# A chunked scan in 64-wide tiles: the level products of the triangular inverse kept inside one layout

## The chip, the core and the metric

The kernel runs on one core of a Trainium2 chip as one program. The metric is the device time of that program in microseconds, the median of the runs; before the change it is 4052.07 us (three runs, 4046.66 to 4060.16).

## The reference, cut to what matters

The program is two stacked blocks of two layers each, in fp32. The odd layer of the first block mixes tokens in two ways, by neighbourhood attention and by a scan; the change lies in the scan alone. The scan runs in both directions over 256 context tokens and then 512 image tokens, for 8 heads with a 64 by 64 state each:

```python
def step(S, inp):
    w_t, k_t, v_t, kk_t, a_t = inp[:5]
    sa = jnp.einsum('bhvk,bhk->bhv', S, kk_t)
    S = (S * w_t[:, :, None, :] - sa[..., None] * (kk_t * a_t)[:, :, None, :]
         + v_t[..., None] * k_t[:, :, None, :])
    return S, (jnp.einsum('bhvk,bhk->bhv', S, inp[5]) if emit else None)
S, ys = lax.scan(step, state0, xs, reverse=reverse)
```

## The kernel before, in words

**Chunks.** The tokens of a direction are cut into 12 chunks of 64 (4 of context, 8 of image tokens); two directions make 24 units, each a Python generator `unit(d, i)`. Within a chunk the recurrence becomes a triangular 64 by 64 system for each head, and its inverse `X` is built in levels: level 0 is a mask and a subtraction, levels 1 to 5 each join blocks of twice the size.

**Layouts.** The 8 heads are three bits. A tile holds one bit in the half of its partitions (64 rows each) and the other two as four groups `g` on the free axis; the layouts "N", "T" and "J" (`LAY`) differ in which bit is in the partitions. `prod(ps, lam, mu, ...)` multiplies 64 by 64 tiles of layout `lam` and leaves the result in layout `mu`, for all 8 heads: the contraction is over one half of the partitions, the result goes to the other bit's half, so that its 8 products go to all four quarters of the array (both row halves and both column halves), and to two PSUM banks, one for each row half. `seen` is the access pattern by which the result is read.

**PSUM.** `pair()` takes the next of three buffers of two banks each (tag `rw`). Whoever takes a buffer waits until the use three calls earlier has been read out. Two further banks (`mm`) serve the other matmuls.

**A unit's steps** (one `yield` ends a step): `A` and `X` at level 0 (L1495 to L1504, two buffers); the products with the decayed keys, `B`, and for image chunks `rb` (L1506 to L1515, two buffers); four transposes of 128 by 128 for `kt` (L1516 to L1524); `bv`; then five levels of two steps each. The first step of a level (L1534 to L1541) transposes `X` (two transposes of 128 by 128, by `ident`, to layout N), multiplies `A` with the columns of `X` that this level needs (32 of 64), copies the transpose to `xt` on ScalarE and the masked product to `w` on VectorE. The second (L1543 to L1549) multiplies `xt` with `w` and subtracts the result from `X`. After the levels come the state's part of `bv` (L1555), `un` (L1559), the new state (L1565), and for image chunks the output `y` (L1578 to L1586).

**Order.** A unit starts every 3 ticks (`EVERY`), a block (the inputs of two chunks, `block(d, g)`, with 8 matmuls at L1447, a scan on VectorE and products on GpSimd) starts 9 ticks ahead of its first unit. In a tick every live unit and block issues one step, oldest first, so some six units are in flight, three or four of them in the levels. All engines issue in this order. In the first 15 ticks three steps of another generator (`more`, the output product of the neighbourhood part) are issued in each tick; near the end the readout of `y` is.

Of the kernel before, what the change touches and what calls it, by code (L numbers as in the profile page):

```python
# [9 lines left out]
F32 = mybir.dt.float32  # L10
F32R = mybir.dt.float32r
AF = mybir.ActivationFunctionType
ALU = mybir.AluOpType
# [3 lines left out]
P = 128  # L17
# [4 lines left out]
T = TX + TC  # L22
# [254 lines left out]
class Prog:  # L277
# [31 lines left out]
    c = v  # L309
# [1054 lines left out]
    def rwkv(self, R, mod, inner, parts, more):  # L1364
# [5 lines left out]
        nc, a = self.nc, self.a  # L1370
        DEC = float(np.exp(-0.5))
        with ExitStack() as es:
            self.psum(es, mm=2)
            pps = self.pool(es, "rwps", 3, space=PSUM)
            up = self.pool(es, "ru", 2)
            lora, mk = R["lora"], R["mk"]
            y = R["y"]
            HALF = (slice(0, 64), slice(64, 128))
            LAY = {"N": (2, 0, 1), "T": (1, 0, 2), "J": (0, 1, 2)}
            i64 = self.c("i64")  # L1380
# [6 lines left out]
            def prod(ps, lam, mu, *terms, base=0, step=64, at=0, n=64):  # L1387

                lb, mb = LAY[lam][0], LAY[mu][0]
                bits = [0, 0, 0]  # L1390
                for bits[3 - lb - mb] in range(2):
                    for i, (L, Rb) in enumerate(terms):
                        for bits[lb] in range(2):
                            for bits[mb] in range(2):
                                g = 2 * bits[LAY[lam][1]] + bits[LAY[lam][2]]
                                h = HALF[bits[lb]]
                                o0 = base + step * bits[3 - lb - mb] + at
                                nc.tensor.matmul(ps[HALF[bits[mb]], bits[lb], o0:o0 + n], L(g)[h], Rb(g)[h],  # L1398
                                                 start=i == 0, stop=i == len(terms) - 1)

            def seen(ps, lam, mu, base=0, step=64, at=0, n=64):

                v = ps[:, :, base:base + 2 * step].rearrange("p b (s w) -> p b s w", s=2)[:, :, :, at:at + n]
                return v if LAY[mu][1] == LAY[lam][0] else v.rearrange("p b s w -> p s b w")
# [2 lines left out]
            two = lambda t_: t_.rearrange("p (x y) w -> p x y w", x=2)  # L1407
            mask = lambda d, i, n=1: (mk[:, d, i:i + n].rearrange("p m q -> p (m q)").unsqueeze(1).unsqueeze(1)
                                      .to_broadcast([P, 2, 2, 64 * n]))
            ident = self.c("ident")  # L1410

            ka = up.tile([P, 2, 4], F32, name="kaff", bufs=1)
            nc.vector.tensor_scalar(out=ka[:, 0], in0=self.v("k_a"), scalar1=0.5, scalar2=None, op0=ALU.mult)
# [70 lines left out]
            def unit(d, i):  # L1484
                ci = chunk(d, i)
                isx = ci >= 4
                E, b_, kd_, gc_, vt = blocks[d, ci // 2]
                c = ci % 2
                e0, e1 = (lambda g: E[:, g, c, 0]), (lambda g: E[:, g, c, 1])
                b, kd, v = (lambda g: b_[:, g, c]), (lambda g: kd_[:, g, c]), (lambda g: vt[:, c, g])  # L1490
                gc = gc_[:, :, c]
                nn = P if isx else 64
                ev = lambda g: E[:, g, c].rearrange("p e t -> p (e t)")[:, :nn]

                ps = pair()  # L1495
                prod(ps, "N", "J", (e0, b))
                A = sm("A", 5)
                nc.scalar.copy(two(A), seen(ps, "N", "J"))
                ps = pair()
                prod(ps, "N", "J", (b, e0))  # L1500
                X = sm("X", 6)
                nc.vector.tensor_tensor(out=two(X), in0=seen(ps, "N", "J"), in1=mask(1 - d, 0), op=ALU.mult)
                nc.vector.tensor_tensor(out=X, in0=i64s, in1=X, op=ALU.subtract)
                yield  # L1504

                ps = pair()  # L1506
                prod(ps, "N", "T", (kd, ev), step=P, n=nn)
                B = sm("B", 6, nn)
                nc.vector.tensor_tensor(out=two(B), in0=seen(ps, "N", "T", step=P, n=nn), in1=mask(d, 6, nn // 64), op=ALU.mult)
                if isx:  # L1510
                    ps = pair()
                    prod(ps, "N", "T", (b, e1))
                    rb = sm("rb", 6)
                    nc.vector.tensor_tensor(out=two(rb), in0=seen(ps, "N", "T"), in1=mask(d, 7), op=ALU.mult)
                yield  # L1515
                if i < 11:  # L1516

                    ps = pair()
                    for q, t_ in enumerate((kd_, b_)):
                        for j in range(2):  # L1520
                            nc.tensor.transpose(ps[:, q, P * j:P * j + P], t_[:, 2 * j:2 * j + 2, c].rearrange("p e t -> p (e t)"), ident)
                    kt = up.tile([P, 2, 4, 64], F32, tag="kt", name="kt", bufs=5)
                    nc.scalar.copy(kt.rearrange("p q g f -> p q (g f)"), ps[:, :, 0:256])
                yield  # L1524
                ps = pair()
                prod(ps, "T", "J", ((lambda g: B[:, g, 0:64]), v))
                bv = sm("bv", 5)
                nc.scalar.activation(out=two(bv), in_=seen(ps, "T", "J"), func=AF.Copy, scale=-1.0)
                yield

                for l in range(1, 6):

                    blk = lambda t_: t_.rearrange("p (n two b) -> p n two b", two=2, b=1 << l)[:, :, 1 - d]
                    ps = pair()  # L1534
                    for e in range(2):
                        nc.tensor.transpose(ps[:, 0, P * e:P * e + P], X[:, 2 * e:2 * e + 2].rearrange("p h c -> p (h c)"), ident)  # L1536
                    prod(ps, "J", "N", (grp(A), (lambda g: blk(X[:, g]))), base=256, step=32, n=32)
                    xt, w = sm("xt", 3), sm("w", 3, 32)
                    nc.scalar.copy(two(xt), ps[:, 0, 0:256].rearrange("p (e j r) -> p j e r", e=2, j=2))
                    m = mk[:, d, l, 0:32].unsqueeze(1).unsqueeze(1).to_broadcast([P, 2, 2, 32])  # L1540
                    nc.vector.tensor_tensor(out=two(w), in0=seen(ps, "J", "N", base=256, step=32, n=32), in1=m, op=ALU.mult)  # L1541
                    yield
                    ps = pair()  # L1543
                    prod(ps, "N", "J", (grp(xt), grp(w)), step=32, n=32)
                    xb = X.rearrange("p (x y) (n two b) -> p x y n two b", x=2, two=2, b=1 << l)[:, :, :, :, 1 - d]
                    s = seen(ps, "N", "J", step=32, n=32).rearrange("p x y (n b) -> p x y n b", b=1 << l)
                    if l == 5:
                        xb, s = xb[:, :, :, 0], s[:, :, :, 0]
                    nc.vector.tensor_tensor(out=xb, in0=xb, in1=s, op=ALU.subtract)  # L1549
                    yield  # L1550

                N = state[d]
                if N is not None:
                    ps = pair()
                    prod(ps, "N", "J", (e0, grp(N)))  # L1555
                    nc.vector.tensor_tensor(out=two(bv), in0=two(bv), in1=seen(ps, "N", "J"), op=ALU.subtract)
                yield
                ps = pair()
                prod(ps, "J", "T", (grp(X), grp(bv)))  # L1559
                un = sm("un", 3)  # L1560
                nc.scalar.copy(two(un), seen(ps, "J", "T"))
                yield
                if i < 11:
                    ps = pair()
                    prod(ps, "T", "N", ((lambda g: kt[:, 0, g]), v), ((lambda g: kt[:, 1, g]), grp(un)))  # L1565
                    N2 = sm("N", 3)
                    gcb = gc.unsqueeze(2).to_broadcast([P, 4, 64])
                    if N is None:
                        nc.vector.tensor_tensor(out=two(N2), in0=seen(ps, "T", "N"), in1=two(gcb), op=ALU.mult)
                    else:  # L1570
                        nc.vector.tensor_tensor(out=two(N2), in0=two(N), in1=seen(ps, "T", "N"), op=ALU.add)
                        nc.vector.tensor_tensor(out=N2, in0=N2, in1=gcb, op=ALU.mult)
                    state[d] = N2
                yield
                if isx:

                    ps = pair()
                    prod(ps, "N", "J", (grp(N), e1))  # L1578
                    prod(ps, "T", "J", (v, (lambda g: B[:, g, 64:P])), (grp(un), grp(rb)), base=P)
                    c4 = ci - 4  # L1580
                    yy = two(y[:, :, 64 * c4:64 * c4 + 64])
                    if (c4 < 4) == (d == 0):
                        nc.scalar.copy(yy, seen(ps, "N", "J"))
                    else:
                        nc.vector.tensor_tensor(out=yy, in0=yy, in1=seen(ps, "N", "J"), op=ALU.add)
                    nc.vector.tensor_tensor(out=yy, in0=yy, in1=seen(ps, "T", "J", base=P), op=ALU.add)  # L1586
                done.add((d, i))
# [881 lines left out]
```

## Time and profile before

| | |
|---|---|
| median of 3 runs | 4052.07 us |
| lowest, highest | 4046.66, 4060.16 us |
| the profiled execution: its time | 4060.4 us |
| its span, first to last instruction | 4058.7 us |
| mean granted TensorE clock | 0.968 of full speed |
| busy, share of the span: TensorE, VectorE, ScalarE, GpSimd | 94%, 58%, 38%, 7% |

The profile is one execution. Lines of the kernel are named L1398 and so on; instructions recorded inside a helper carry the helper's line, so all products of `prod` stand at L1398 and are told apart by the tiles that they write and read (`rw<-X,A` writes a buffer of the tag `rw` and reads `X` and `A`). An fp32 product is recorded as two matmuls, each with its own weight load, so 8 heads give 16 records; an fp32 transpose is one. A record's length includes the way through the array, which overlaps with the next record; the pace is the distance between starts.

### The profile page before, as it was taken

To read this page: it belongs to the slowest core of one execution; us is meant where nothing else is said; L and a number is where in the kernel's file an instruction comes from. 1 tells how busy PE (TensorE), PEld (TensorE's weight loads), DVE (VectorE), ACT (ScalarE), POOL (GpSimd) and SP (SyncE) were. 2 spreads that over 40 slices of the span, in tenths; PEclk is the share of its full clock that TensorE was granted. 3 is DMA by queue.
4 is the path that set the end of the run, shared out by engine and by line. 5 is a ranking of instruction groups with operands and counts; after the bars stand their busy time and mean duration, and the time that the engine had idled before them with its cause. 6 is when DMAs were issued, how large, how long until landed. Compare 5 with 4: busy or idle time off the path is not lost.

```text
span 4058.7 us, 68289 instructions
## 1 busy us (share of the span) xinstructions
PE 3832.5 (94%) x28564; PEld 3110.9 (77%) x28564; DVE 2348.8 (58%) x4086; ACT 1554.3 (38%) x2862; POOL 294.7 (7%) x310
## 2 busy tenths in 40 slices
PE   7999999999999898899999999999998999989998
PEld 5667788888877676678877877888887777767887
DVE  6556555545645455577664466455458788784334
ACT  4456321212445344342233333212126576663222
POOL 0222000000010011000000000000001222120000
PEclk8999999999999979999999998999998999999999
DMA  4221133333214311145541102333333233322232
GB/s 176 85 84 41 63 110 116 115 107 100 75 50 140 117 42 40 31 147 177 165 146 60 65 30 72 116 116 116 102 96 122 82 108 109 120 73 83 94 95 87
DMA packets 144196, 393.08 MB, mean 97 GB/s; under 512 B 14096, under 2 KB 45712, under 8 KB 142992
## 3 DMA queue, kind: packets, MB, share of 16 engines
q1 hardware_dynamic: 143888, 388.72, 29.0%
q8 instruction: 224, 3.67, 0.4%
q14 instruction: 84, 0.69, 0.1%
HBM read 374.38 MB, written 14.29 MB: 96 GB/s over the span
## 4 chain that ended last, share of the span: by engine, by line
PE 80%; DVE 9%; issue 4%; ACT 4%; DMA 1%; POOL 1%; SPq 0%; DVEq 0%; ACTq 0%; POOLq 0%
PE mm L418 18%; PE mm L359 15%; PE mm L361 15%; PE mm L363 15%; PE mm L388 4%; PE rw L1398 2%; PE y L900 2%; PE tp L887 2%; PE y L2342 1%; PE rw L1536 1%; DVE cva L2068 1%; DVE wlo L340 1%; PE s L817 1%; ACT whi L339 1%; PE s L818 0%
## 5 line engine op out<-in xcount | busy, mean ns | idle before, releaser
L339 ACT CAST whi<-w 128x1024 fp32r<-128x1024 f32 (+2 forms) x429 | 439.1, 1025 | 1588.0 <-PE mm L361 1004.3
L340 DVE TENSOR_TENSOR wlo<-w,whi 128x1024 fp32r<-128x1024 f32 (+2 forms) x429 | 518.0, 1208 | 329.9 <-ACT whi L339 321.2
L359 PE MATMUL mm<-fhi,whi 128*128 128x512 f32 x2016 | 610.0, 356 | 0.0
L361 PE MATMUL mm<-flo,whi 128*128 128x512 f32 x2016 | 609.4, 356 | 0.0
L363 PE MATMUL mm<-fhi,wlo 128*128 128x512 f32 x2016 | 607.5, 355 | 0.0
L363 PEld LDWEIGHTS mm<-fhi,wlo 128*128 128x128 f32 x2016 | 331.3, 187 | 61.3
L359 PEld LDWEIGHTS mm<-fhi,whi 128*128 128x128 f32 x2016 | 331.4, 187 | 60.8
L361 PEld LDWEIGHTS mm<-flo,whi 128*128 128x128 f32 x2016 | 331.4, 187 | 59.4
L475 DVE SCALAR_TENSOR_TENSOR wdot<-wmod,cb 128x1024 f32<-128x1024 f32 x288 | 352.0, 1222 | 9.6 <-ACT cb L469 3.6
L626 DVE SCALAR_TENSOR_TENSOR x<-mm,mod,x 128x512 f32<-128x512 f32 (+1 forms) x214 | 131.9, 643 | 339.4 <-PE mm L363 270.2
L738 DVE TENSOR_TENSOR g<-g,mm 128x512 f32<-128x512 f32 (+1 forms) x134 | 75.6, 590 | 403.4 <-PE mm L363 395.7
L359 PE MATMUL mm<-ah,whi 128*128 128x512 f32 x972 | 294.0, 356 | 0.0
L361 PE MATMUL mm<-al,whi 128*128 128x512 f32 x972 | 293.8, 356 | 0.0
L363 PE MATMUL mm<-ah,wlo 128*128 128x512 f32 x972 | 293.0, 355 | 0.7 <-DVE wlo L340 0.7
L363 PEld LDWEIGHTS mm<-ah,wlo 128*128 128x128 f32 x972 | 159.7, 187 | 30.6 <-DVE wlo L340 1.1
L359 PEld LDWEIGHTS mm<-ah,whi 128*128 128x128 f32 x972 | 159.7, 187 | 29.4
L361 PEld LDWEIGHTS mm<-al,whi 128*128 128x128 f32 x972 | 159.7, 187 | 28.8
L838 POOL TENSOR_SCALAR p<-p,st 128x256 f32<-128x256 f32 (+3 forms) x128 | 95.7, 748 | 1008.9 <-DVE st L837 917.7
L418 PE MATMUL mm<-shi,whi 128*128 128x512 f32 x328 | 138.8, 423 | 0.0
L418 PE MATMUL mm<-shi,wlo 128*128 128x512 f32 x328 | 131.1, 401 | 2.9 <-DVE wlo L340 2.9
L418 PE MATMUL mm<-slo,whi 128*128 128x512 f32 x328 | 131.9, 402 | 0.0
L2068 DVE SCALAR_TENSOR_TENSOR cva<-cvb,v_ssd,cva 128x512 f32<-128x512 f32 (+1 forms) x176 | 121.7, 704 | 11.7 <-ACT cva L2066 9.6
(573 smaller groups left out, 7339.9 us busy)
## 6 DMA issues: line engine op xcount, KB each, us to landing
wmod<-wmod SPq DMA_DIRECT2D x176, 512.0 KB, 3.8
w<-wfi SPq DMA_DIRECT2D x176, 512.0 KB, 3.3
w<-ws_in SPq DMA_DIRECT2D x62, 512.0 KB, 3.3
w<-wfo SPq DMA_DIRECT2D x64, 448.0 KB, 3.4
w<-wfo SPq DMA_DIRECT2D x32, 512.0 KB, 3.5
rb<-acd SPq DMA_DIRECT2D x32, 512.0 KB, 3.9
w<-wo_in SPq DMA_DIRECT2D x26, 512.0 KB, 3.3
w<-wa_in SPq DMA_DIRECT2D x21, 512.0 KB, 3.3
```

What stands on the lines that cost most here:

```text
L339: self.nc.scalar.copy(hi, src)
L340: (engine or self.nc.vector).tensor_tensor(out=lo, in0=src, in1=hi.bitcast(F32), op=ALU.subtract)
L359: nc.tensor.matmul(o, whi(k), ah(k), start=s, stop=False)
L361: nc.tensor.matmul(o, whi(k), al(k), start=False, stop=False)
L363: nc.tensor.matmul(o, wlo(k), ah(k), start=False, stop=e)
L388: self.nc.tensor.matmul(o, w[:, k], x[:, k, t0:t0 + n], start=s, stop=e)
L418: self.nc.tensor.matmul(o, w[:, k], x[:, k, t0:t0 + n], start=s, stop=e)
L475: dot = nc.vector.scalar_tensor_tensor(out=t, in0=w, scalar=1.0, in1=cb[:, i], op0=ALU.mult, op1=ALU.mult, accum_out=out[:, j, i:i + 1])
L626: self.nc.vector.scalar_tensor_tensor(out=x, in0=ps, scalar=mod[:, i_g + m, i:i + 1], in1=x, op0=ALU.mult, op1=ALU.add)
L838: nc.gpsimd.tensor_scalar(out=p, in0=p, scalar1=l, scalar2=1.0, op0=ALU.mult, op1=ALU.mult)
L887: nc.tensor.transpose(ps[:, k * P:k * P + P], p[:, (k0 + k) * P:(k0 + k + 1) * P], self.c("ident"))
L2068: nc.vector.scalar_tensor_tensor(out=acc, in0=pc[:, t:t + n], scalar=w(t), in1=acc, op0=ALU.mult, op1=ALU.add)
```

## The change

Two new functions replace the transposes and the level products. `turn` multiplies 64 by 64 tiles with the 64 by 64 identity `i64`, from one layout to another, over all four quarters of the array. `within` multiplies inside a layout: partitions 0 to 63 contract into output partitions 0 to 63 and 64 to 127 into 64 to 127, with all 8 results side by side in one bank; without a right operand it multiplies with the identity.

```
+            def turn(ps, lam, mu, L, base=0, step=64, at=0):
+                lb, mb = LAY[lam][0], LAY[mu][0]
+                bits = [0, 0, 0]
+                for bits[3 - lb - mb] in range(2):
+                    for bits[lb] in range(2):
+                        for bits[mb] in range(2):
+                            h = HALF[bits[lb]]
+                            o0 = base + step * bits[3 - lb - mb] + at
+                            nc.tensor.matmul(ps[HALF[bits[mb]], bits[lb], o0:o0 + 64],
+                                             L(2 * bits[LAY[lam][1]] + bits[LAY[lam][2]])[h], i64[h], start=True, stop=True)
+            def within(ps, L, R, n):
+                for g in range(4):
+                    for h in HALF:
+                        o = ps[h, n * g:n * g + n]
+                        if R is None:
+                            nc.tensor.matmul(o, L(g)[h], i64[h], start=True, stop=True)
+                        else:
+                            nc.tensor.matmul(o, L(g)[h], R(g)[h], start=True, stop=True)
```

`A` and `X` of level 0 share one buffer, and VectorE reads it first; `B` and `rb` share one buffer; `kt` comes from 16 products with the identity instead of four transposes:

```
                 prod(ps, "N", "J", (e0, b))
-                A = sm("A", 5)
+                prod(ps, "N", "J", (b, e0), base=P)
+                A, X = sm("A", 5), sm("X", 6)
+                nc.vector.tensor_tensor(out=two(X), in0=seen(ps, "N", "J", base=P), in1=mask(1 - d, 0), op=ALU.mult)
                 nc.scalar.copy(two(A), seen(ps, "N", "J"))
-                ps = pair()
-                prod(ps, "N", "J", (b, e0))
...
                 prod(ps, "N", "T", (kd, ev), step=P, n=nn)
+                if isx:
+                    prod(ps, "N", "T", (b, e1), base=256)
...
-                    ps = pair()
-                    prod(ps, "N", "T", (b, e1))
...
-                    for q, t_ in enumerate((kd_, b_)):
-                        for j in range(2):
-                            nc.tensor.transpose(ps[:, q, P * j:P * j + P], t_[:, 2 * j:2 * j + 2, c].rearrange("p e t -> p (e t)"), ident)
+                    turn(ps, "N", "T", kd, step=P)
+                    turn(ps, "N", "T", b, step=P, at=64)
```

In a level the transpose of `X` goes to bank 0 of its buffer and the product of `A` to bank 1; the second product goes to bank 0. `xt`, `w` and `X` stay in layout J:

```
-                    for e in range(2):
-                        nc.tensor.transpose(ps[:, 0, P * e:P * e + P], X[:, 2 * e:2 * e + 2].rearrange("p h c -> p (h c)"), ident)
-                    prod(ps, "J", "N", (grp(A), (lambda g: blk(X[:, g]))), base=256, step=32, n=32)
+                    within(ps[:, 0], grp(X), None, 64)
+                    within(ps[:, 1], grp(A), (lambda g: blk(X[:, g])), 32)
...
                     ps = pair()
-                    prod(ps, "N", "J", (grp(xt), grp(w)), step=32, n=32)
+                    within(ps[:, 0], grp(xt), grp(w), 32)
```

The access patterns of the copies and of the subtraction follow the new places; their sizes and engines stay.

## Rows read from the trace of the kernel before

**Rows 1.** The page: the chain that ended last, shares by line.
```profile
PE mm L418 18%; PE mm L359 15%; PE mm L361 15%; PE mm L363 15%; PE mm L388 4%; PE rw L1398 2%; PE y L900 2%; PE tp L887 2%; PE y L2342 1%; PE rw L1536 1%; DVE cva L2068 1%; DVE wlo L340 1%; PE s L817 1%; ACT whi L339 1%; PE s L818 0%
```
**Rows 2.** Windows of the scan: us, busy us (count) by engine, clock, DMA.
```profile
1475.00:1672.00 197.00, 170.68 (x5764) 139.18 (x5768) 118.51 (x331) 82.58 (x216) 15.52 (x22) 0.96 0.13 35
1672.00:1708.00 36.00, 29.70 (x1070) 22.64 (x1067) 22.18 (x68) 14.99 (x37) 0.00 (x0) 1.00 0.11 31
```
**Rows 3.** Groups by line in 1391 to 1708 us: busy us, mean ns, idle before.
```profile
L1398 PE MATMUL rw<-X,A 64*64 64x32 f32 x1920 | 56.5, 233 | 1.8 <-issue 1.7
L1536 PE MATMUL rw<-consts,X 128*128 128x128 f32 x240 | 55.8, 317 | 15.6 <-DVE x L1586 10.7 <-DVE X L1502 3.4 <-ACT un L1561 0.7
```
**Rows 4.** Timeline, TensorE, one unit's period: start us, length us, instruction, idle before.
```profile
1485.01 0.46 PE L1398 MATMUL rw<-E,b 64*64 64x64 f32 x16 [0.38 <-DVE w L1541]
...
1487.80 0.65 PE L1398 MATMUL rw<-E,kd 64*64 64x128 f32 x16
1488.26 0.29 PE L1398 MATMUL rw<-E,b 64*64 64x64 f32 x6
1489.05 0.38 PE L1398 MATMUL rw<-E,b 64*64 64x64 f32 x9 [0.50 <-issue]
...
1490.98 0.44 PE L1521 MATMUL rw<-consts,kd 128*128 128x128 f32 x2
1491.25 0.38 PE L1521 MATMUL rw<-consts,b 128*128 128x128 f32 x2
1491.57 0.46 PE L1398 MATMUL rw<-bv,X 64*64 64x64 f32 x16
1491.96 0.44 PE L1536 MATMUL rw<-consts,X 128*128 128x128 f32 x2
1492.32 0.43 PE L1398 MATMUL rw<-X,A 64*64 64x32 f32 x16
1492.58 0.41 PE L1398 MATMUL rw<-w,xt 64*64 64x32 f32 x16
1492.92 0.44 PE L1536 MATMUL rw<-consts,X 128*128 128x128 f32 x2
...
1493.81 0.41 PE L1398 MATMUL rw<-b,E 64*64 64x64 f32 x16
1494.60 0.46 PE L1398 MATMUL rw<-E,b 64*64 64x64 f32 x16 [0.38 <-DVE w L1541]
```
**Rows 5.** Timeline of another layer: products of one row half, two column halves.
```profile
2378.98 0.68 PE L1922 MATMUL tp<-qd,kn 64*64 64x64 f32 x18
```
**Rows 6.** Timeline of another layer: 32 moving columns, 128 weight columns.
```profile
3083.52 1.08 PE L2042 MATMUL tp<-dta,c_ssd 128*128 128x32 f32 x8 [0.33 <-DVE dta L2032]
3084.44 1.06 PE L2042 MATMUL tp<-dta,consts 128*128 128x32 f32 x8
```
**Rows 7.** Waits in 1391 to 1708 us: total us, times, longest us.
```profile
DVE w L1541 <- ACT xt L1539: 30.5, 46, 1.5
PE rw L1536 <- DVE x L1586: 10.7, 12, 1.3
PE rw L1398 <- DVE w L1541: 10.3, 25, 1.1
```
**Rows 8.** Timeline, ScalarE and VectorE, end of that period.
```profile
1493.85 0.37 ACT L1539 COPY xt<-rw 128x256 f32<-128x256 f32 x1 [0.59 <-PE rw L1398]
1494.25 0.29 DVE L1541 TENSOR_TENSOR w<-rw,rmask 128x128 f32<-128x128 f32 x1 [0.68 <-ACT xt L1539]
```
**Rows 9.** The instructions of two lines: duration ns, least, median, most.
```profile
L1509 DVE TENSOR_TENSOR B<-rw,rmask x24: 412/681/693, 1405.8 to 1672.9; 128x512 f32<-128x512 f32 x16, 128x256 f32<-128x256 f32 x8
L1514 DVE TENSOR_TENSOR rb<-rw,rmask x16: 415/415/425, 1489.5 to 1673.4; 128x256 f32<-128x256 f32 x16
```
**Rows 10.** Windows of the scan at the lower clock, and their sum.
```profile
1428.80:1452.60 23.80, 23.80 (x483) 19.32 (x483) 10.62 (x30) 8.44 (x21) 0.73 (x2) 0.50 0.13 36
...
sum 47.60, PE 47.60 PEld 38.99 DVE 21.80 ACT 15.68 POOL 3.02; mean PE 11.90 PEld 9.75 DVE 5.45 ACT 3.92 POOL 0.75
```

More of the change, by code (lines that the diff above doesn't have):

```diff
@@ L1409, in rwkv @@
                                       .to_broadcast([P, 2, 2, 64 * n]))
-            ident = self.c("ident")
             ka = up.tile([P, 2, 4], F32, name="kaff", bufs=1)
@@ L1496, in unit @@
                 prod(ps, "N", "J", (e0, b))
-                A = sm("A", 5)
+                prod(ps, "N", "J", (b, e0), base=P)
+                A, X = sm("A", 5), sm("X", 6)
+                nc.vector.tensor_tensor(out=two(X), in0=seen(ps, "N", "J", base=P), in1=mask(1 - d, 0), op=ALU.mult)
                 nc.scalar.copy(two(A), seen(ps, "N", "J"))
-                ps = pair()
-                prod(ps, "N", "J", (b, e0))
-                X = sm("X", 6)
-                nc.vector.tensor_tensor(out=two(X), in0=seen(ps, "N", "J"), in1=mask(1 - d, 0), op=ALU.mult)
                 nc.vector.tensor_tensor(out=X, in0=i64s, in1=X, op=ALU.subtract)
@@ L1510, in unit @@
                 if isx:
-                    ps = pair()
-                    prod(ps, "N", "T", (b, e1))
                     rb = sm("rb", 6)
-                    nc.vector.tensor_tensor(out=two(rb), in0=seen(ps, "N", "T"), in1=mask(d, 7), op=ALU.mult)
+                    nc.vector.tensor_tensor(out=two(rb), in0=seen(ps, "N", "T", base=256), in1=mask(d, 7), op=ALU.mult)
                 yield
@@ L1518, in unit @@
                     ps = pair()
-                    for q, t_ in enumerate((kd_, b_)):
-                        for j in range(2):
-                            nc.tensor.transpose(ps[:, q, P * j:P * j + P], t_[:, 2 * j:2 * j + 2, c].rearrange("p e t -> p (e t)"), ident)
-                    kt = up.tile([P, 2, 4, 64], F32, tag="kt", name="kt", bufs=5)
-                    nc.scalar.copy(kt.rearrange("p q g f -> p q (g f)"), ps[:, :, 0:256])
+                    turn(ps, "N", "T", kd, step=P)
+                    turn(ps, "N", "T", b, step=P, at=64)
+                    kt = sm("kt", 5, P)
+                    nc.scalar.copy(two(kt), seen(ps, "N", "T", step=P, n=P))
                 yield
@@ L1534, in unit @@
                     ps = pair()
-                    for e in range(2):
-                        nc.tensor.transpose(ps[:, 0, P * e:P * e + P], X[:, 2 * e:2 * e + 2].rearrange("p h c -> p (h c)"), ident)
-                    prod(ps, "J", "N", (grp(A), (lambda g: blk(X[:, g]))), base=256, step=32, n=32)
+                    within(ps[:, 0], grp(X), None, 64)
+                    within(ps[:, 1], grp(A), (lambda g: blk(X[:, g])), 32)
                     xt, w = sm("xt", 3), sm("w", 3, 32)
-                    nc.scalar.copy(two(xt), ps[:, 0, 0:256].rearrange("p (e j r) -> p j e r", e=2, j=2))
-                    m = mk[:, d, l, 0:32].unsqueeze(1).unsqueeze(1).to_broadcast([P, 2, 2, 32])
-                    nc.vector.tensor_tensor(out=two(w), in0=seen(ps, "J", "N", base=256, step=32, n=32), in1=m, op=ALU.mult)
+                    nc.scalar.copy(xt, ps[:, 0, 0:256].rearrange("p (g c) -> p g c", g=4))
+                    nc.vector.tensor_tensor(out=w, in0=ps[:, 1, 0:128].rearrange("p (g c) -> p g c", g=4),
+                                            in1=mk[:, d, l, 0:32].unsqueeze(1).to_broadcast([P, 4, 32]), op=ALU.mult)
                     yield
                     ps = pair()
-                    prod(ps, "N", "J", (grp(xt), grp(w)), step=32, n=32)
-                    xb = X.rearrange("p (x y) (n two b) -> p x y n two b", x=2, two=2, b=1 << l)[:, :, :, :, 1 - d]
-                    s = seen(ps, "N", "J", step=32, n=32).rearrange("p x y (n b) -> p x y n b", b=1 << l)
+                    within(ps[:, 0], grp(xt), grp(w), 32)
+                    xb = X.rearrange("p g (n two b) -> p g n two b", two=2, b=1 << l)[:, :, :, 1 - d]
+                    s = ps[:, 0, 0:128].rearrange("p (g n b) -> p g n b", g=4, b=1 << l)
                     if l == 5:
-                        xb, s = xb[:, :, :, 0], s[:, :, :, 0]
+                        xb, s = xb[:, :, 0], s[:, :, 0]
                     nc.vector.tensor_tensor(out=xb, in0=xb, in1=s, op=ALU.subtract)
@@ L1564, in unit @@
                     ps = pair()
-                    prod(ps, "T", "N", ((lambda g: kt[:, 0, g]), v), ((lambda g: kt[:, 1, g]), grp(un)))
+                    prod(ps, "T", "N", ((lambda g: kt[:, g, 0:64]), v), ((lambda g: kt[:, g, 64:P]), grp(un)))
                     N2 = sm("N", 3)
```

## The prediction, made before the change was run

> **What bounds the kernel now.** I read the page first. In its chain by line [rows 1] the matmuls of the large projections lead, and the scan is small: L1398 has 2% and L1536 1%. So the change is worth what it is worth inside the scan, which lasts from about 1391 to 1708 us, 317 us of 4058.7, and nothing after it moves except by starting sooner or later. A change of less than 0.3% of the whole, 12 us, could not be told from no change by such runs; that is 4% of the scan.
>
> The windows of the scan [rows 2] show TensorE with a record running for 170.7 of 197 us in the middle, VectorE for 118.5 and ScalarE for 82.6. Only TensorE is near its limit, but its records overlap, so I went on to the timeline of TensorE for one unit's period without block work [rows 4]. The products of two successive units' level-0 `X` start at 1485.01 and 1494.60, so a unit takes 9.59 us. Between them starts follow each other at fixed distances, with a few waits that can be named. The reader is to see that the scan goes at the pace at which TensorE issues, plus some waits for PSUM buffers. The groups by line [rows 3] give the size: the transposes of `X` and the products of `A` and `X` have 56 us of records each. So what counts is the pace of each group of products (start to start), and which waits go.
>
> **The price of a level now.** From rows 4: the transposes start at 1491.96, the product with `A` at 1492.32, the second product at 1492.58, the next transposes at 1492.92. That is 0.36 + 0.26 + 0.34 = 0.96 us for the two steps of a level, with what it costs to go between 128-wide and 64-wide instructions inside it (the second product takes 0.34 when a transpose follows, the first 0.26 when a product follows, so some 0.08 of it is the change of shape).
>
> **The price of a level afterwards.** All three groups become 16 records of 64 by 64 on two quarters of the array, since `within` contracts the lower half into the lower half and the upper into the upper; `prod` uses four. The trace of before has no such diagonal pair. The nearest row is L1922 [rows 5]: there a run of 18 records has one row half and both column halves, two quarters as well. They take 0.68 us; less some 0.23 for the length of one record (the mean of the 64-wide ones, [rows 3]) that is 0.45 over 17 distances, 0.0265 us each. In `prod` the pace is 0.26/16 = 0.016 us [rows 4]. So two quarters are nearly half as fast as four. That only 32 columns stream in two of the three groups doesn't help: in [rows 6] eight records with 32 moving columns and 128 weight columns take 0.92 us from start to start, 0.115 each, which is the weight load's time, not that of the columns. Half the weight columns would be 0.0575 for a quarter, and with two quarters at work 0.029 for each record. I take 0.028, between 0.0265 and 0.029: 0.45 us a group, 1.35 a level. Each level then costs TensorE 0.39 us more, and there are 24 units of 5 levels: 120 * 0.39 = +47 us. The bounds are 3 * 16 * 0.0265 = 1.27 and 3 * 16 * 0.029 = 1.39, so +37 to +52.
>
> **`kt`.** Its four transposes start at 1490.98 and the next product at 1491.57, 0.59 us, with 0.08 more ahead for the change of shape. Its 16 products with the identity go over four quarters and stream as many columns as the product with `kd` and 128 columns, which takes from 1487.80 to 1488.26, 0.46. That is -0.21 for 22 units, -5 us.
>
> **Waits that go.** In the period of rows 4 three kinds are seen. The second product of level 0 (`rw<-E,b`) starts 0.79 after the first, where 0.26 would do: its buffer is still being read by `w`, which came after `xt`, because both were in the same banks (the VectorE instruction starts when ScalarE's has ended, [rows 8]). Over the scan `w` waited 30.5 us for `xt` [rows 7]. After the change `w` reads a bank of its own and the second product shares the first one's buffer, so this 0.5 goes, in 24 units. The product for `rb` stops for about 0.55 in its middle (1488.26 to 1489.05, less what six records need); it gets no buffer of its own any more, so this goes too, in 16 units. Some 0.5 us of small waits, what the starts of the period leave over, are filled by the longer groups between a read and the reuse.
>
> **Waits that come.** `B` and `rb` now hold one buffer until both VectorE instructions, 0.68 and 0.415 us [rows 9], have read it, and the third buffer after it is asked for after only 0.23 + 0.45 us of products; with the way through the array of 0.2 and a start of 0.1 that leaves a wait of about 0.7, in 16 units. What is queued behind it is all of the older units' level work, since TensorE issues in order. `A`'s copy now comes after the mask of `X` on VectorE in the same banks, 0.4 later than before; the next buffer but two is asked for after 0.47 + 0.45, which leaves about 0.35, in 24 units. So 0.5 * 24 + 0.55 * 16 = 21 us go and 0.7 * 16 + 0.35 * 24 = 20 come; with the small ones, 0.5 * 24 = 12, the waits are worth about -13. The bounds are nothing, and the whole 30.5 us that `w` waited.
>
> **Elsewhere in the scan.** Where block work delays VectorE, TensorE stands still whatever it has to do: 10.7 us over 12 waits for the readout of `y` [rows 7]. Longer products ahead of such a wait fill a part of it: -4. In the drain of the last units, 36 us [rows 2], a unit's own chain sets the pace. There `xt` is copied while the product with `A` still runs and `w` no longer follows `xt`, which gives back what the longer groups cost; so of the +42 the drain's share, 36/317, is taken off: -5. The access patterns of the copies change but their sizes don't: nothing, hidden behind TensorE; if TensorE's cover were gone, it would still be nothing, since the other engines do the same instructions on as many elements.
>
> **Sum.** 47 - 5 - 13 - 4 - 5 = +20 us. Against the profiled execution's own 4060.4 us (a span of 4058.7 and 1.7 around it) that is 4080; that execution was 8.3 above the median of the runs, so against the median, 4052.07, it is 4072. The bounds together: 37 - 5 - 30 - 4 - 5 = -7, and 52 - 5 = +47: 4045 to 4099.
>
> **Rivals.**
>
> First, faster: the pace of two diagonal quarters is that of four. The two quarters of rows 5 share their row half; a diagonal pair shares nothing. At 0.016 a record a level is 0.77 and not 0.96: 120 * -0.19 = -23, with -5 and -13 some -41, 4011 us. The point from which it decides: with the other terms at -27 the levels must cost less than +27, so 1.18 us a level, 0.0246 a record. Against it: rows 6, where one weight load alone takes 0.115 for 128 columns. Chance 0.12.
>
> Second, no change: the added work falls into idle time. TensorE has no record for 26 of the 197 us in the middle [rows 2], and waits for `w` alone are 10.3 us [rows 7]. If every wait that TensorE has were filled, the sum would be near nothing: 4052. Against it: the waits that come. Chance 0.10.
>
> Third, no change through the clock. [...] Chance 0.08. [...]
>
> Fourth, much slower: both row halves now write the same bank at once, into different partitions, which no product of the trace does (`prod` gives each row half its own bank). If the array took them one after the other, a record would cost 0.0575 (half of that in [rows 6]), a level 2.76, 120 * 1.8 = +216: 4052 + 216 - 5 - 13 = 4250. For and against it no row speaks. [...] Chance 0.08.
>
> **How the numbers follow.** The forecast itself has 0.62, with its own range of 4045 to 4099; about a sixth of that, 0.10, lies within 12 us of the median. So slower by over 0.3%: 0.52 + 0.08 = 0.60; within 0.3%: 0.10 + 0.10 + 0.08 = 0.28; faster: 0.12. The first and the fourth rival, 0.20, stay outside the range; the others lie in it: 4044 to 4102.
>
> **What would show it.** Right: 16 records of `within` start over 0.42 to 0.46 us, a unit's period without block work is about 10.8 us and not 9.6, `w` starts without a wait for `xt`, a wait of half a microsecond or more follows `rb`, and the scan lasts some 337 us. Wrong: `within` at 0.25 (first rival) or 0.9 (fourth), a period below 9.8 (second), low-clock stretches gone (third). The weakest step is the balance of the waits, each of which rests on one period; the largest is the pace on two quarters.

## The result, and the profile after

The changed kernel takes 4098.38 us (median of 4 runs, 4092.95 to 4100.62) against 4049.53 for the kernel before in the same session (4046.66 to 4060.16). The ratio is 1.0114, with a 95% interval of 1.0092 to 1.0136: 46 us slower, 37 to 55. The forecast was slower by 20, with 4102 as its upper end.

The page of the kernel after, its chain by line (the answer to [rows 1]):

```profile
PE mm L418 17%; PE mm L359 14%; PE mm L361 14%; PE mm L363 14%; PE mm L388 4%; PE y L900 2%; PE rw L1421 2%; PE tp L887 2%; PE y L2359 1%; PE rw L1419 1%; PE rw L1398 1%; DVE wlo L340 1%; DVE cva L2085 1%; PE s L817 1%; ACT whi L339 1%
```

L1419 and L1421 are the two lines of `within`, L1410 is `turn`. Windows of the scan (as [rows 2], with the drain in 1708 to 1746 us), then the low-clock stretches (as [rows 10]):

```profile
1475.00:1672.00 197.00, 173.91 (x6296) 163.43 (x6297) 103.20 (x284) 77.98 (x199) 17.15 (x24) 1.00 0.12 35
1672.00:1708.00 36.00, 31.11 (x1210) 29.00 (x1208) 17.62 (x54) 8.06 (x23) 0.00 (x0) 1.00 0.02 4
1708.00:1746.00 38.00, 34.08 (x1137) 29.89 (x1136) 19.91 (x63) 14.27 (x36) 0.00 (x0) 1.00 0.10 29
...
sum 10.20, PE 10.13 PEld 9.72 DVE 3.27 ACT 1.39 POOL 0.62; mean PE 5.07 PEld 4.86 DVE 1.63 ACT 0.70 POOL 0.31
```

From the first copy of `A` to the last of `un` the scan lasted 304.3 us before (1403.2 to 1707.5) and 345.8 after (1399.9 to 1745.7). These 41.5 us are the whole difference of the two spans, 40.2. Groups by line of the scan after (1386 to 1750 us, as [rows 3]):

```profile
L1419 PE MATMUL rw<-c_odd,X 64*64 64x64 f32 x1920 | 84.7, 224 | 13.4 <-DVE x L1603 5.5 <-ACT A L1521 2.9 <-issue 2.7
L1421 PE MATMUL rw<-w,xt 64*64 64x32 f32 x1920 | 79.5, 219 | 6.1 <-DVE w L1557 2.0 <-issue 1.9 <-DVE rb L1533 1.7
L1421 PE MATMUL rw<-X,A 64*64 64x32 f32 x1920 | 77.9, 217 | 2.2 <-issue 2.1
```

In place of 240 transposes there are 1920 records, and one level product has 78 us of records where it had 56. Timeline of TensorE after, a level between undisturbed neighbours (as [rows 4]):

```profile
1498.85 0.65 PE L1419 MATMUL rw<-c_odd,X 64*64 64x64 f32 x16
1499.31 0.62 PE L1421 MATMUL rw<-X,A 64*64 64x32 f32 x16
1499.75 0.65 PE L1421 MATMUL rw<-w,xt 64*64 64x32 f32 x16
1500.22 0.67 PE L1419 MATMUL rw<-c_odd,X 64*64 64x64 f32 x16
```

The starts lie 0.46, 0.44 and 0.47 us apart: 1.37 for a level that took 0.96 [rows 4], 0.029 a record. In the trace's records such a group goes in pairs, two starts in every 58 ns, without a stop. Last the waits after, in 1386 to 1750 us (as [rows 7]):

```profile
ACT xt L1556 <- PE rw L1421: 135.2, 98, 4.0
...
DVE w L1557 <- ACT xt L1556: 37.6, 38, 1.8
ACT A L1521 <- DVE X L1520: 20.6, 23, 2.1
```

And `w` on VectorE in the timeline after (as [rows 8]):

```profile
1495.01 0.29 DVE L1557 TENSOR_TENSOR w<-rw,rmask 128x128 f32<-128x128 f32 x1 [1.28 <-ACT xt L1556]
```

`w` still starts when `xt` has been copied, though each now reads a bank of its own, and `xt` still starts behind the product with `A` (L1421), not behind the identity products (L1419). The copy of `A` has a new wait, for the mask of `X`.

### The profile page after: what moved, and what is told of

Same layout as the page of the kernel before. It is cut to its first block, busy times and chain, and to the rows that moved or that the text cites. A ratio compares the mean times of both kernels' runs of the same rounds, so it can differ in the third digit from the quotient of the medians.

```text
span 4098.9 us, 72892 instructions
## 1 busy us (share of the span) xinstructions
PE 3869.2 (94%) x30860; PEld 3178.7 (78%) x30860; DVE 2347.8 (57%) x4086; ACT 1556.3 (38%) x2862; POOL 295.3 (7%) x310
## 4 chain that ended last, share of the span: by engine, by line
PE 80%; DVE 9%; issue 4%; ACT 4%; DMA 2%; POOL 1%; SPq 0%; DVEq 0%; ACTq 0%; POOLq 0%
PE mm L418 17%; PE mm L359 14%; PE mm L361 14%; PE mm L363 14%; PE mm L388 4%; PE y L900 2%; PE rw L1421 2%; PE tp L887 2%; PE y L2359 1%; PE rw L1419 1%; PE rw L1398 1%; DVE wlo L340 1%; DVE cva L2085 1%; PE s L817 1%; ACT whi L339 1%
```

## The experiments

The mean granted clock of an execution says much about its time. Over all 99 executions of the kernels below and of the kernel before beside them, a line fitted to each execution's distance from its own kernel's mean gives 2.2 us more for every 0.001 less of mean clock (correlation -0.85). So the table has both: the difference of medians to the kernel before in the same session, the difference of the mean clocks, and what is left at 2.2 us per 0.001. The line was fitted within kernels; that it holds between two kernels is assumed. The brackets below the table are ratios of means, so their differences can be 1 or 2 us from those of the medians here.

| kernel | records added | difference, us | clock | left, us |
|---|---|---|---|---|
| e1 levels alone | 1680 | +41 | +0.0017 | +45 |
| e2 all but the levels | 616 | +15 | -0.0049 | +4 |
| e3 all, levels by `turn` | 2296 | +41 | -0.0043 | +31 |
| e4 the change, a tile of its own for `w` | 2296 | +49 | +0.0010 | +51 |
| e5 transposes of `X` by `turn` alone | 1680 | +25 | -0.0021 | +20 |
| e6 `kt` alone | 616 | +15 | -0.0039 | +6 |
| e7 merged tiles alone | 0 | +3 | -0.0021 | -1 |
| e8 second product in bfloat16 | -960 | -24 | 0.0000 | -24 |
| e9 second product twice | 1920 | +45 | -0.0028 | +39 |
| e10 the change without `kt` | 1680 | +29 | +0.0045 | +39 |
| e11 both products in bfloat16 | -1920 | -39 | -0.0015 | -42 |

**e1 and e2: the change cut in two.** e1 has the levels' part of the diff on the kernel before; e2 has everything else of it (one tile for `A` and `X`, one for `B` and `rb`, and `kt`):

```
e1:  +  within(ps[:, 0], grp(X), None, 64)
     +  within(ps[:, 1], grp(A), (lambda g: blk(X[:, g])), 32)
     +  within(ps[:, 0], grp(xt), grp(w), 32)
e2:  +  prod(ps, "N", "J", (b, e0), base=P)
     +  prod(ps, "N", "T", (b, e1), base=256)
     +  turn(ps, "N", "T", kd, step=P)
     +  turn(ps, "N", "T", b, step=P, at=64)
```

> Only the level products go through `within`; `kt` and the buffers of level 0 and of `B` and `rb` are as before. The pace theory (two quarters of the array give a record each 29 ns, so 120 levels cost TensorE 0.44 us more) expects the whole loss here: 40 to 55 us slower than before. The waits theory (the common buffers of `A` and `X` and of `B` and `rb` make new waits) expects less than 30 here.

Measured: 1.0101 [1.0083, 1.0120], 41 us slower. The levels cost about what the pace says.

> The reverse: level products as before, `kt` by `turn`, common buffers for `A` and `X` and for `B` and `rb`. The pace theory expects 5 to 20 us faster than before (four transposes less for `kt`, two buffers less per unit). The waits theory expects 10 us or more slower.

Measured: 1.0038 [1.0023, 1.0052], 15 us slower where the prediction's terms say faster. Its failure lies in this half.

**e3 and e4: four quarters for the transposes of `X`, and a buffer of its own for the product with `A`.** e3 has the levels as before, but `turn` for the transposes, and the rest of the change; e4 is the change with the product that `w` reads in a buffer of its own:

```
e3:  -  for e in range(2): nc.tensor.transpose(ps[:, 0, P * e:P * e + P], ...)
     +  turn(ps, "J", "N", grp(X))
e4:  +  p2 = pair()
     +  within(p2[:, 1], grp(A), (lambda g: blk(X[:, g])), 32)
```

> The kernel after, but in the levels the transposes of `X` are products with the identity over all four quarters (`turn` from J to N), and both products go from J to N and back over four quarters as before the change. The pace theory expects 16 records in about 0.25 us each time, a level of 0.75 us against 0.96 before, and the kernel 20 to 40 us faster than before, 4010 to 4030. If what costs is not the number of quarters but products with the identity in place of transposes (16 records and 16 weight loads for 2), it expects no gain over before.

Measured: 1.0097 [1.0079, 1.0115], 41 us slower, a clear miss: on four quarters the groups are fast (0.23 to 0.31 us from one start to the next, 1488.37 to 1489.48 in the timeline below), and the kernel isn't. The trace says why. The waits of TensorE in the scan of e3 (1390 to 1755 us):

```profile
PE rw L1398 <- issue: 27.4, 31, 1.7
PE rw L1398 <- DVE w L1559: 18.1, 14, 2.1
PE rw L1398 <- DVE E L1498: 13.3, 1, 13.3
PE rw L1410 <- issue: 12.0, 12, 1.6
```

"issue" means that it waited for nothing that the profile shows; before, such waits of L1398 were 4.1 us in all. The timeline of e3 shows where they stand:

```profile
1486.53 0.34 PE L1398 MATMUL rw<-bv,X 64*64 64x64 f32 x6
1487.47 0.38 PE L1398 MATMUL rw<-bv,X 64*64 64x64 f32 x9 [0.60 <-issue]
...
1488.37 0.47 PE L1410 MATMUL rw<-c_odd,X 64*64 64x64 f32 x16
1488.65 0.40 PE L1398 MATMUL rw<-X,A 64*64 64x32 f32 x16
1488.96 0.46 PE L1398 MATMUL rw<-vt,B 64*64 64x64 f32 x16
1489.25 0.41 PE L1398 MATMUL rw<-b,E 64*64 64x64 f32 x16
1489.48 0.28 PE L1398 MATMUL rw<-E,b 64*64 64x64 f32 x5
1491.09 0.39 PE L1398 MATMUL rw<-E,b 64*64 64x64 f32 x10 [1.33 <-issue]
...
1493.44 0.26 PE L1398 MATMUL rw<-X,A 64*64 64x32 f32 x5
1494.83 0.36 PE L1398 MATMUL rw<-X,A 64*64 64x32 f32 x10 [1.14 <-issue]
```

Groups stop in their middle. Counted over all the lines, 127 matmuls start between the first stop and the second and 128 between the second and the third, each with its weight load: 256 instructions. The DMA queues of e3 in 1480 to 1510 us:

```profile
q8 instruction: 8, 0.13, 1.8%
```

Eight packets of 16384 bytes in 30 us; for 256 instructions that is 64 bytes each. In the trace's DMA records those from 1480 to 1495 us start at 1481.59, 1485.13, 1488.60 and 1492.20 and take about 1.1 us, and each of the three stops ends 1.3 to 1.4 us after a packet has landed. From 1480 to 1700 us of every run two packets start no closer than 3.27 us, in e3 3.62 apart in the median. In the kernel before and after, too, a packet goes with 128 products and their loads: from 1480 to 1700 us 127.6 and 128.0 matmuls start from one packet to the next, in the mean. So 128 records with their loads took 3.3 us at least and 3.6 in the median of e3, 0.026 to 0.028 each, where e3's groups of 16 on four quarters, at 0.23 to 0.31 us, have 0.014 to 0.019 a record. I call it the supply. All the "issue" waits of e3's scan end 1.2 to 1.6 us after such a packet has landed. The 0.029 of `within` is another matter: its even 58 ns for two records show no stop, so I take it for the array's pace; it lies just above the 0.026 to 0.028 of the supply.

> The kernel after, with the product of `A` in a buffer of its own, so that `w` and `xt` read different buffers, and `xt` can be copied while that product runs; everything on TensorE is as after. The pace theory expects the kernel after within 8 us. If the wait of `w` for `xt` inside the common buffer is what keeps the gain away, 15 us or more faster than the kernel after. A loss would say that three buffers are too few for one more user in each level.

Measured: 1.0120 [1.0100, 1.0139], 49 us slower, as the change. In its trace the groups of a level start at 1495.01, 1495.48 and 1495.97 us, 0.47 and 0.49 apart, as with a shared tile, and `w` has no wait for `xt` any more. So that wait, 37.6 us in the change, costs nothing that shows, unless the one more buffer in each level takes back what its end gives. Both row halves of a group still write one bank in e4, so it doesn't test the fourth rival.

**e5 to e8: the supply against the pace and the waits.** Each is one edit on the kernel before: `turn` for the transposes of `X` (e5), the change's `kt` (e6), the merged tiles (e7), and

```
e8:  +  xt = up.tile([P, 4, 64], mybir.dt.bfloat16, ...)
     +  w = up.tile([P, 4, 32], mybir.dt.bfloat16, ...)
```

> The kernel before with one edit: in a level the two transposes become 16 records of products with the identity that cross over between the layouts, so they run on all four quarters; everything else stays. Supply theory: TensorE's instructions arrive in blocks of 16 KB (256 instructions, so 128 weight loads and 128 products), and in none of the runs so far did two blocks of the scan come closer than 3.28 us, which is 0.026 us for each record with its load, on whatever quarters it runs; 14 more records in each of 120 levels are 1680 x 0.026 = 44 us, less what now falls into waits: 25 to 45 us slower. Pace theory: the group takes 0.23 us on four quarters where the two transposes took 0.37 to 0.42, so 120 levels give 16 to 22 us back: 10 to 22 us faster.

Measured: 1.0063 [1.0040, 1.0085], 25 us slower, 20 at equal clock. The pace theory has the wrong sign; the supply has it right, at its lower end. TensorE's "issue" waits of L1398 and L1410 in its scan are 27.7 and 4.0 us, where the kernel before has 4.1 in all.

> The kernel before with the change's kt alone: four transposes become 32 records of products with the identity, 22 times; nothing else changes. Supply theory: 616 more records x 0.026 us = 16 us, less what falls into waits: 8 to 18 us slower, so that it explains nearly all of the 15 us that the merges and kt together cost. Waits theory (the merged buffers of A, X, B and rb cost those 15 us): kt by itself is within 5 us of the kernel before, or faster by up to 5.

Measured: 1.0036 [1.0019, 1.0053], 15 us slower, the whole of e2. The supply theory's number is met, but not its mechanism: the trace of e6 has 2.2 us of "issue" waits of TensorE. Some 9 us go with the clock, whose mean was 0.9684 over 10 executions against 0.9723 over 20 of the kernel before.

> The kernel before with the merged buffers alone: A and X in one PSUM tile, B and rb in one PSUM tile, and A copied after X is masked; no record of TensorE is added or taken away. Supply theory: nothing to pay, 13 us faster to 4 us slower. Waits theory (A's copy behind the mask of X, B's mask behind both products): 8 to 15 us slower.

Measured: 1.0007 [0.9992, 1.0022], the same. The merged tiles neither cost the 15 us of e2 nor bring what the prediction gave them.

> The kernel before with xt and w rounded to bfloat16 as they are copied out of PSUM, so that the second product of a level is 8 records in place of 16; the result is less exact for it. Supply theory: 960 records fewer x 0.026 us = 25 us: 12 to 28 us faster. Pace theory: 8 records x 0.0145 us fewer in each of 120 levels, 14 us, and part of it falls into waits for w: 0 to 14 us faster.

Measured: 0.9943 [0.9922, 0.9964], 24 us faster at the same clock: 0.025 us for each record taken away. That is the supply's number, but it doesn't show the supply. The records that are left are quicker, which neither theory reckoned with: the timeline of e11 below has a group of 8 in bfloat16 at 0.09 us, and at 0.17 before a transpose, where 16 in fp32 take 0.26 and 0.34 [rows 4]. So a group is 0.17 us shorter, 20 us over 120 levels, without any stop; the "issue" waits that could go were 4.1 us, and the trace of e8 has none.

**e9 to e11: more records, the change without `kt`, and fewer records.**

```
e9:     prod(ps, "N", "J", (grp(xt), grp(w)), step=32, n=32)
     +  prod(ps, "N", "J", (grp(xt), grp(w)), base=256, step=32, n=32)
e11: +  A = up.tile([P, 4, 64], mybir.dt.bfloat16, ...)
     -  lambda g: blk(X[:, g])
     +  lambda g: blk(X[:, g].bitcast(mybir.dt.bfloat16).rearrange("p (c k) -> p c k", k=2)[:, :, 1])
```

e10 is the change with the four transposes for `kt` back; e11 stands on e8.

> The kernel before with the second product of a level issued twice, the second time into unused columns of the same tile that nothing reads: 16 more records on four quarters in each of 120 levels and nothing else. Supply theory: 1920 x 0.026 us = 50 us, less what falls into waits: 30 to 52 us slower. Pace theory: a group of 16 takes 0.23 us on four quarters, 28 us in all: 15 to 28 us slower.

Measured: 1.0115 [1.0098, 1.0131], 45 us slower, 39 at equal clock, beyond the pace's 28. So 16 records on four quarters, which start over 0.23 us, cost 0.33 to 0.38 us in a level. Its trace has 11.0 us of "issue" waits of TensorE in the scan against 4.1, so most of the loss is the pace, and of the 11 to 17 us beyond it some 7 are seen as the supply.

> The change without its kt: the levels within their layout and the merged tiles of A and X, B and rb stay, the four transposes for kt come back (616 records fewer than with the change). Supply theory: 8 to 16 us less than the change, so 30 to 40 us slower than the kernel before. The prediction's own term (the change's kt saves 5 us): 5 us more than the change, 50 us or more slower than the kernel before.

Measured: 1.0075 [1.0060, 1.0090], 30 us slower, 16 less than the change. `kt` costs inside the change what it costs alone, though the difference of two runs is uncertain by some 11; the prediction's own term said the opposite sign.

> The kernel before with both products of a level in bfloat16: xt, w and A rounded to it as they are copied out of PSUM, and X read as the upper halves of its numbers, so that a level has 8 + 8 + 2 records in place of 16 + 16 + 2; the result is less exact for it. Supply theory: another 960 records gone, 20 to 25 us beyond the 23 us that the half gave: 38 to 52 us faster than the kernel before. If after the first half the waits of the two chains set the scan: 23 to 32 us faster.

Measured: 0.9908 [0.9891, 0.9926], 37 us faster than the kernel before and the fastest of all, for inputs of the level products rounded to bfloat16. The second step brought about 15 us for 960 records. The timeline of e11 has the lengths of its groups:

```profile
1512.60 0.44 PE L1558 MATMUL rw<-consts,X 128*128 128x128 f32 x2
1512.97 0.24 PE L1398 MATMUL rw<-X,A 64*64 64x32 bf16 x8
1513.06 0.22 PE L1398 MATMUL rw<-w,xt 64*64 64x32 bf16 x8
1513.23 0.44 PE L1558 MATMUL rw<-consts,X 128*128 128x128 f32 x2
```

At 0.17 us a level the shorter groups alone would bring 20 us, as in e8, so neither run tells the supply from a shorter group; e3 and e5 do. From 1480 to 1700 us e11 has 38 packets of instructions where the kernel before has 51 and e3 58. They start 4.9 us apart in the median, and TensorE has no "issue" wait in its scan, so the supply doesn't press there.

## Why the prediction was right and wrong

The sign, the mechanism named first and the range, at its very end, were right; the size was less than half. The terms against the runs, in the order in which e1, e10 and the change add them up:

- **Levels, +47** (with the -4 and -5 taken off elsewhere, +38): measured +41 (e1), and by e1's trace also 1.37 us a level (groups start at 1484.34, 1484.81, 1485.25, 1485.71). The price of 0.028 a record on two quarters was 0.029. Right in size.
- **Merged tiles, -13:** +3 alone (e7, -3 to +9) and about -11 on top of the levels (e10 less e1, each uncertain by 6 to 8; -6 at equal clock). The number can stand, but in part by luck, for its parts were mixed. Right: the second product of level 0 starts 0.23 us behind the first (1477.98 and 1478.21 in the trace after), not 0.79. Wrong: `w` was to start without a wait for `xt`; it waited 37.6 us, more than the 30.5 of [rows 7]. The waits that come were forecast at 20 us of TensorE and are 2.9 for `A`'s copy and 1.7 for `rb`. And the 0.55 * 16 = 9 us that the product for `rb` was to get back were misread: its stop at 1489.05 in [rows 4] is marked "issue", stands in the middle of a group and ends 1.45 us after a packet of instructions has landed. It was the supply and no buffer, the one such stop in that product, and "issue" waits grew from 4.1 us to 10.5 with the change.
- **`kt`, -5: the step that failed.** Measured +15 alone (e6) and +16 in the change (e10 against it): 20 of the 26 us that the forecast lacks. The working says "its 16 products with the identity" and prices them by 16 records of the product with `kd`, 0.46 us, because they stream as many columns. Sixteen fp32 products are 32 records, and the paragraph on the levels had just set the weight load, not the columns, as the price of a record. In e6 they start at 1492.52 and the next product at 1493.11 us:

```profile
1492.52 0.44 PE L1410 MATMUL rw<-c_odd,kd 64*64 64x64 f32 x16
1492.78 0.41 PE L1410 MATMUL rw<-c_odd,b 64*64 64x64 f32 x16
1493.11 0.46 PE L1398 MATMUL rw<-bv,X 64*64 64x64 f32 x16
```

That is 0.59, just what the four transposes take in [rows 4], so no more was to be had than the 0.08 ahead of them, -2 us. With -2 to 0 in place of -5 the sum is 23 to 25. The other 15 us and more no term of the prediction holds: 616 more records, and a lower clock. In e6 some 9 us go with the clock and 6 don't; in the change against e10 the clock (0.9748 and 0.9768) accounts for 4 of 16. The supply doesn't show in e6 (2.2 us of "issue" waits against 4.1 before); in the change it can be some 4 us (10.5 against 6.4 in e10). What the rest is and why these products come with a lower clock stays open; neither was tried by itself.

**The rivals.** The first (two quarters as fast as four) fell with the pace of 0.029. Its deeper assumption, that four quarters at 0.016 a record would have made the kernel faster, fell too: e3 and e5 have their transposes of `X` on four quarters and are slower, with 39 and 32 us of "issue" waits, because the instructions arrived at 0.026 to 0.028 us a record. The prediction weighed TensorE's columns, its weight loads and its waits, but not its instructions. The second (the added work falls into idle time) failed: the records take more than the idle time had. The third (no change, through the clock) was half right: in the profiled execution the low-clock time of the scan fell from 47.6 us [rows 10] to 10.2, and e1 and e10 run at a higher mean clock than the kernel before. It was worth about 4 us in e1 and 10 in e10, less than the 24 that half of the 47.6 us at a clock of 0.50 would be, and lay beside +45 and +39. These are means over executions; the two profiled ones, at 0.968 and 0.975, differ by more. Where products replace transposes the mean clock did not move one way: it rose with `within` (e1 +0.0017) and fell with `turn` (e5 -0.0021, e6 -0.0039). In e7, which replaces no transpose, it fell by 0.0021 too, so only the largest of these say much, e6 and the +0.0045 of e10, and they differ in sign. The fourth (the row halves take turns in one bank, at 0.0575 a record) is refuted by the 0.46 us of a group, half of what it asks. For two row halves that write different partitions of one bank no cost shows here: the 0.029 a record lies within the 0.0265 to 0.029 that were worked out for two quarters from [rows 5] and [rows 6].

**The signs named.** The 0.42 to 0.46 of a `within` group were 0.44 to 0.47; the scan grew by 41.5 us, not 20, and a unit's period, from one copy of `A` to the next (starts at 1479.6, 1491.2 and 1502.8 us), was 11.6 us and not 10.8. In the first of these the timeline after has two stops of the supply:

```profile
1486.50 0.38 PE L1398 MATMUL rw<-bv,X 64*64 64x64 f32 x9 [0.31 <-issue]
1490.24 0.39 PE L1398 MATMUL rw<-E,b 64*64 64x64 f32 x10 [0.49 <-issue]
```

The wait behind `rb` shows as 1.7 us over the scan in L1421's row above, not 0.7 in each of 16 units.

## What to carry to other kernels

Count instructions, not calls: one fp32 product here is two matmuls and two weight loads, so a 128-wide transpose traded for four 64-wide products (8 records) multiplies by eight what TensorE must be fed (240 records became 1920), however well they pack the array. In a stretch of short records, compare the records with what the instruction queue brings. In e3 it brought a block of 256 instructions every 3.6 us in the median and none sooner than 3.3 after the one before, while the array could take one every 1.9 by an estimate from e9's 0.23 us for 16 records (128 at 0.0145); there, as in e5, a better packing of the array brought nothing. A group that stops in its middle with "issue" is the sign to look for; the rows of the kernel before had one, and it was read as a wait for a buffer. e8 and e11, with fewer records, were faster, but their records were quicker as well. Before you credit or blame an edit for 10 us, look at the mean granted clock of the executions on both sides.

## What the runs showed of the hardware that was not expected

TensorE ran out of instructions: in e3 39 us of the scan went in "issue" waits, 43 of them, nearly all in the middle of a group, that end 1.2 to 1.6 us after a 16384-byte packet of the instruction queue has landed. And a mean clock that differs by 0.004 between two kernels, as e6 and the kernel before do (0.9684 and 0.9723), goes with 9 us in 4050 by the line fitted above, 2.2 us for 0.001, as much as a small edit is worth.
